# Thirty-six elementwise differences moved from VectorE to GpSimd in a fused MLP kernel

**Chip and metric.** One core of one Trainium2 chip. The metric is the device time of one execution in microseconds (us). All runs told here were in the fast state, save the single run of the last experiment, whose state is unknown; where a time is given, it is the median of a kernel's runs.

## The reference

Eight batches of 1024 rows go through two matrix products with a tanh GELU between them:

```python
# x: 8 x 1024 x 1024, w1: 1024 x 4096, w2: 4096 x 1024, all float32
h = x @ w1
h = 0.5 * h * (1 + np.tanh(np.sqrt(2 / np.pi) * (h + 0.044715 * h ** 3)))
return (h @ w2).astype(np.float32)
```

## The kernel before

The kernel works on blocks of 1024 rows (`sb` 0 to 7), in fp16, and computes both products by a Strassen-like scheme with seven products in place of eight. In a block, `matmul1` (m1) makes the GELU values `g` in four tiles, g11, g12, g21 and g22; the second matmul then needs sums and differences of these tiles, the first of which, g11 - g21, is made in m1, written over g21, two chunks (a "pair", `j`) at a time. A "later m1" is that of `sb` 2 to 7, in which two of the seven products are split once more ("inner").

Cut to what the change and the argument touch:

```python
def tt(out, in0, in1, op, pin=False):            # line 119 in every profile
    i = nc.vector.tensor_tensor(out=out, in0=in0, in1=in1, op=op)
    if pin:
        tc.keep_in_program_order(i)
...
        def add(out, in1, in0=None):             # in1 is a PSUM bank
            tt(out, out if in0 is None else in0, in1, ADD, True)
...
        def difference(j):
            if j >= 0:
                cs = slice(2 * j, 2 * j + 2)
                tt(g["21"][:, cs], g["11"][:, cs], g["21"][:, cs], SUB, True)
...
        def steady(j):
            ...   # pairs 0 to 3: GpSimd copies a mark from g11 ("pace"), then issues the loads of the next x
            if sb > 1 and j == 5:                # "early": a part of the second matmul, on GpSimd
                early[7] = gcp.tile([P, NI // 2, HT // 2], GT, name="gc")
                u, v = (inner_block(g["22"], b) for b in ("11", "21"))
                nc.gpsimd.tensor_tensor(out=early[7], in0=u, in1=v, op=SUB)
...
        for j in range(NI // 2):                 # 8 pairs
            ...   # products 1 and 2; gelu "21" of the pair before, on ScalarE
            for h in range(2):
                add(a[h], banks_b[h])
            difference(j - 1)
            ...   # products 5, 6, 3, 7, their adds and gelus
            steady(j)
        difference(NI // 2 - 1)
```

## Time and profile before

| | before |
|---|---|
| time, median of the three runs (range) | 1487.91 us (1487.71 to 1488.25) |
| TensorE (PE) busy | 1477.3 of 1486.0 us |
| VectorE (DVE) busy | 1149.5 us |
| GpSimd (POOL) busy | 231.8 us |
| one pair of a later m1, difference to difference | 11.73 us |
| VectorE busy in a later m1, from its first inner matmul to the second matmul (mean of six) | 61.7 of 86.9 us |

The line to read first is TensorE's: what is not 1477.3 us is mostly start-up.

How the rows read: a row in order of time has the start and the duration in us, engine, line, operation, output<-inputs, shapes, how many instructions are merged in it (x5), and in brackets the idle time of the engine in front of it and what ended that. A row of a list of waits has the total in us, how many times, and the longest. A row of the chain (the work that ended last, followed back) has only start, duration, engine, tile and line. L119 is the helper `tt`, so the tiles tell its rows apart; g is fp16 in SBUF, tmp fp32 in SBUF, ps a bank of PSUM.

### The profile page before, as it was taken

The page shows a single profiled execution, that of the slowest core. Times are in us where ns is not written, and L with a number is a line of the kernel's source. Part 1 is how long each engine was busy: PE and PEld are TensorE (multiplying, and loading weights), DVE is VectorE, ACT ScalarE, POOL GpSimd, SP SyncE. Part 2 cuts the span into 40 slices and gives each one's busy share as a digit, 9 for nine tenths or more (in the row PEclk, how much of TensorE's full clock was granted, in tenths as well). Part 3 has the DMA queues.
Part 4 walks back from the last instruction along what each step waited for, and adds up shares of the span by engine and source line. Part 5 has one row for each costly group of instructions (what it writes and reads, how often), then busy time and mean ns, then how long its engine had stood idle before and what let it go on. Part 6 is the DMA issues. An engine that isn't in the chain of part 4 may idle for free.

```text
span 1486.0 us, 26324 instructions
## 1 busy us (share of the span) xinstructions
PE 1477.3 (99%) x9879; PEld 964.2 (65%) x9879; DVE 1149.5 (77%) x1792; ACT 613.3 (41%) x1154; POOL 231.8 (16%) x311
## 2 busy tenths in 40 slices
PE   9999999999999999999999999999999999999998
PEld 5444444444455787558875588655886568855687
DVE  6657458767677898779987799877997779877887
ACT  5665026621166412663136621366214652056510
POOL 2542222222211012100022001210111101101011
PEclk9999999999999999999999999999999999999999
DMA  9999798987997999989999899998999989997886
GB/s 331 340 355 404 202 363 291 405 269 228 383 288 173 358 306 308 336 203 386 303 307 340 222 364 307 311 305 244 353 305 321 307 263 340 294 373 240 297 279 212
DMA packets 242719, 453.70 MB, mean 305 GB/s; under 512 B 80672, under 2 KB 85792, under 8 KB 241696
## 3 DMA queue, kind: packets, MB, share of 16 engines
q1 hardware_dynamic: 215680, 358.69, 71.6%
q0 software_dynamic: 26912, 93.34, 21.3%
q8 instruction: 77, 1.26, 0.3%
q14 instruction: 50, 0.41, 0.1%
HBM read 355.47 MB, written 111.15 MB: 314 GB/s over the span
## 4 chain that ended last, share of the span: by engine, by line
PE 97%; DVE 1%; DMA 1%; issue 0%; ACT 0%; DVEq 0%
PE ps L438 49%; PE ps L902 35%; PE ps L943 13%; PE ps L368 1%; DVE tmp L119 1%; DMA out_dram<-tmp 0%; PE ps L345 0%; DMA u<-in_x_dram 0%; DVE u L119 0%; ACT u L135 0%; ACT tmp L135 0%; PE ps L303 0%; DVE tmp L337 0%; DVE u L356 0%; DVEq L119 0%
## 5 line engine op out<-in xcount | busy, mean ns | idle before, releaser
L438 PE MATMUL ps<-u 128*128 128x512 f16 (+1 forms) x4104 | 746.7, 344 | 2.3 <-DVE tmp L119 2.3
L119 DVE TENSOR_TENSOR tmp<-tmp,ps 128x256 f32<-128x256 f32 (+1 forms) x930 | 450.7, 532 | 273.9 <-PE ps L438 169.4
L438 PEld LDWEIGHTS <-u 128*128 128x128 f16 x4104 | 401.1, 98 | 345.3 <-issue 11.0
L135 ACT COPY tmp<-ps 128x512 f32<-128x512 f32 x410 | 231.3, 581 | 302.1 <-PE ps L438 154.1
L451 ACT ACTIVATE g<-tmp 128x512 f16<-128x512 f32 x378 | 238.1, 633 | 165.2 <-DVE tmp L119 165.0
L902 PE MATMUL ps<-u,gc 128*128 128x256 f16 x2688 | 300.4, 273 | 0.0
L902 PEld LDWEIGHTS <-gc 128*128 128x128 f16 x2688 | 262.5, 98 | 31.2
L902 PE MATMUL ps<-u,g 128*128 128x256 f16 x2016 | 227.9, 273 | 0.0
L119 DVE TENSOR_TENSOR u<-u 128x2048 f16<-128x2048 f16 (+3 forms) x292 | 219.5, 790 | 9.2 <-DMA raw_d<-u 2.5
L135 ACT COPY u<-ps 128x512 f32<-128x512 f32 (+1 forms) x134 | 77.9, 587 | 348.9 <-PE ps L902 341.4
L902 PEld LDWEIGHTS <-g 128*128 128x128 f16 x2016 | 197.3, 98 | 24.1
L689 POOL DMA_DIRECT2D out_dram<-u x70 | 64.0, 989 | 710.5 <-issue 366.0
L119 DVE TENSOR_TENSOR u<-u,ps 128x512 f32<-128x512 f32 x216 | 147.7, 684 | 34.7 <-PE ps L902 28.5
L943 PE MATMUL ps<-u,g 128*128 128x512 f16 x768 | 166.4, 379 | 0.0
L943 PEld LDWEIGHTS <-g 128*128 128x128 f16 x768 | 75.1, 98 | 90.6
L119 DVE TENSOR_TENSOR g<-g,g 128x2048 f16<-128x2048 f16 (+1 forms) x136 | 130.3, 980 | 1.6 <-ACT g L451 1.6
L119 DVE TENSOR_TENSOR gc<-g,gc 128x2048 f16<-128x2048 f16 x84 | 102.4, 1219 | 0.6
L119 DVE TENSOR_TENSOR gc<-g 128x2048 f16<-128x2048 f16 x78 | 95.0, 1218 | 0.0
L451 ACT ACTIVATE g<-ps 128x512 f16<-128x512 f32 x134 | 79.9, 597 | 13.9 <-PE ps L438 6.9
L138 POOL CAST u<-gc 128x1024 f16<-128x1024 f32 x40 | 47.2, 1190 | 64.7 <-DMA gc<-in_w_dram 61.7
L415 POOL COPY pace<-g 128x2 f16<-128x2 f16 x24 | 4.4, 185 | 191.4 <-ACT g L451 191.4
L536 POOL TENSOR_TENSOR gc<-g 128x2048 f16<-128x2048 f16 x6 | 24.4, 4063 | 62.1 <-ACT g L451 62.1
(37 smaller groups left out, 257.3 us busy)
## 6 DMA issues: line engine op xcount, KB each, us to landing
u<-w_d SPq DMA_DIRECT2D x336, 256.0 KB, 6.5
u<-in_d SPq DMA_DIRECT2D x168, 512.0 KB, 7.1
u<-raw_d SPq DMA_DIRECT2D x252, 256.0 KB, 7.1
out_dram<-u POOLq DMA_DIRECT2D x70, 512.0 KB, 9.3
gc<-in_w_dram SPq DMA_DIRECT2D x48, 512.0 KB, 6.3
u<-in_d SPq DMA_DIRECT2D x96, 256.0 KB, 7.4
raw_d<-u SPq DMA_DIRECT2D x32, 512.0 KB, 8.9
u<-raw_d SPq DMA_DIRECT2D x32, 512.0 KB, 14.1
```

The costliest lines, as they stand in the source:

```text
L119: i = nc.vector.tensor_tensor(out=out, in0=in0, in1=in1, op=op)
L135: tc.keep_in_program_order(nc.scalar.copy(out=out, in_=in_))
L138: pool_last[0] = nc.gpsimd.tensor_copy(out=out, in_=in_)
L368: tc.keep_in_program_order(nc.tensor.matmul(bank[:, cols], lhsT=w[:, k, :], rhs=self.xs.blocks[f"{a}{r}"][:, k, cols], start=r == 1 and k ...
L415: mark = nc.gpsimd.tensor_copy(out=pace, in_=g_chunk[:, :2])
L438: tc.keep_in_program_order(nc.tensor.matmul(bank, lhsT=w, rhs=x, start=first and k == 0, stop=k == n - 1, skip_group_check=not first,))
L451: gelu_last[0] = nc.scalar.activation(out=g[b][:, c, :], in_=src, func=GELU)
L536: nc.gpsimd.tensor_tensor(out=early[7], in0=u, in1=v, op=SUB)
L689: return nc.gpsimd.dma_start(out=rows, in_=src, **kw)
L902: tc.keep_in_program_order(nc.tensor.matmul(bank[:, i * OH // 2:(i + 1) * OH // 2], lhsT=t[:, c, i * P:(i + 1) * P], rhs=self.y[j][:, c, : ...
L943: tc.keep_in_program_order(nc.tensor.matmul(pair(bank), lhsT=a[:, c, :], rhs=chunks(pieces[c // QC])[:, :, c % QC, :], start=(first and c ...
```

## The change

The intent: VectorE is the busiest engine behind TensorE, GpSimd is nearly idle in the later m1, so six of the eight differences of such an m1 go to GpSimd. The last two stay, since the second matmul starts right behind them.

```diff
         def difference(j):
             if j >= 0:
                 cs = slice(2 * j, 2 * j + 2)
-                tt(g["21"][:, cs], g["11"][:, cs], g["21"][:, cs], SUB, True)
+                if sb > 1 and j < NI // 2 - 2:
+                    tc.keep_in_program_order(nc.gpsimd.tensor_tensor(
+                        out=g["21"][:, cs], in0=g["11"][:, cs], in1=g["21"][:, cs], op=SUB,
+                    ))
+                else:
+                    tt(g["21"][:, cs], g["11"][:, cs], g["21"][:, cs], SUB, True)
```

## The prediction

> **What bounds the kernel now.** I read the page's first section first, then the chain that ended last, then the waits of TensorE alone, then the later first matmuls (m1) instruction by instruction. The first section and the list of TensorE's waits:
>
> ```profile
> PE 1477.3 (99%) x9879; PEld 964.2 (65%) x9879; DVE 1149.5 (77%) x1792; ACT 613.3 (41%) x1154; POOL 231.8 (16%) x311
> ```
> ```profile
> PE ps L438 <- DVE tmp L119: 2.3, 7, 0.6
> PE ps L303 <- DVE warm L1027: 1.2, 1, 1.2
> PE ps L345 <- DVE tmp L337: 0.7, 1, 0.7
> PE ps L368 <- ACT u L135: 0.6, 1, 0.6
> ```
>
> TensorE is taken for 1477.3 of 1486.0 us, and in the whole execution it waits for VectorE (DVE) 2.3 us in seven places; the other rows belong to the start-up. The chain says the same: 97% of it is PE, 1% is DVE. A busy TensorE need not be at its best rate, so I worked out a floor from two stretches of the chain that hold one width only:
>
> ```profile
> 208.71 96.69 PE ps L438 x448
> ...
> 856.80 85.63 PE ps L902 x784
> ```
>
> 448 matmuls of 512 columns in 96.69 us are 0.2158 us each; 784 of 256 columns in 85.63 us are 0.1092 us each. In the later m1 (sb 2 to 7) one pair of chunks is five plain products (2 chunks x 4 matmuls of 512 columns: 40 in all) and two inner ones (7 parts x 2 matmuls of 256 columns: 28 in all), which agrees with the 68 weight loads per pair that the timeline shows. At those rates a pair takes 40 x 0.2158 + 28 x 0.1092 = 11.69 us. The differences themselves give the period that is kept, since one comes per pair. On VectorE, in the m1 that runs from about 762 to 857 us:
>
> ```profile
> 801.06 2.40 DVE L119 TENSOR_TENSOR tmp<-tmp,ps 128x256 f32<-128x256 f32 x5 [0.95 <-PE ps L438]
> 803.38 0.68 DVE L119 TENSOR_TENSOR g<-g,g 128x1024 f16<-128x1024 f16 x1
> 804.69 0.42 DVE L119 TENSOR_TENSOR tmp<-tmp,ps 128x256 f32<-128x256 f32 x1 [0.63 <-ACT tmp L135]
> ...
> 812.79 2.40 DVE L119 TENSOR_TENSOR tmp<-tmp,ps 128x256 f32<-128x256 f32 x5 [0.95 <-PE ps L438]
> 815.11 0.68 DVE L119 TENSOR_TENSOR g<-g,g 128x1024 f16<-128x1024 f16 x1
> 816.42 0.42 DVE L119 TENSOR_TENSOR tmp<-tmp,ps 128x256 f32<-128x256 f32 x1 [0.63 <-ACT tmp L135]
> ```
>
> The period is 815.11 - 803.38 = 11.73 us, so 0.04 us of a pair is above the floor. Over 8 pairs x 6 such m1 that is about 2 us, all that any change to VectorE in this stage could win. The second thing in these rows matters more: behind each difference VectorE is idle for 0.63 us, waiting for a ScalarE copy. The add behind the difference does not start earlier if the difference is gone.
>
> **What the Trainium skill says.** The page "GPSIMD Engine Reference", section "3.1 Elementwise — side-by-side cycle accounting", gives 4497 ns on GpSimd against 2293 ns on VectorE for an add of 2048 fp32 elements. This trace has a GpSimd subtraction of that length in fp16 (line 536, the early part of the second matmul), and it takes 4063 ns, so a tenth less; VectorE takes 1219 ns for 2048 fp16 elements, so here the gap is more than three to one. The page "SBUF — State Buffer", section "Who interferes with whom", says that a VectorE instruction with two SBUF inputs contends with a GpSimd instruction that reads SBUF, whichever starts first blocking the other completely, while a VectorE instruction with at most one SBUF input does not contend (outside its two-port modes). The trace agrees with the harmless half:
>
> ```profile
> 810.02 4.06 POOL L536 TENSOR_TENSOR gc<-g 128x2048 f16<-128x2048 f16 x1 [3.29 <-ACT g L451]
> ```
>
> It lies from 810.02 to 814.08 us, across VectorE's adds at 811.42 and 812.79. These have one input in SBUF (tmp) and one in PSUM (ps), and they keep the 0.42 and 2.40 us of the pair before, quoted above. No VectorE instruction with two SBUF inputs falls into it, so nothing here shows the blocking half.
>
> **The change part by part.** Removed from VectorE: pairs 0 to 5 of each of six m1, 36 instructions at 0.684 us (that is what all of them take), 24.6 us. VectorE's sum goes from 1149.5 to about 1125, from 1792 to 1756 instructions. None of it is on the path, by the 0.63 us of idle time behind each.
>
> Added to GpSimd (POOL): 36 subtractions of 1024 elements. Half of line 536's 4063 ns is 2.03 us; with something fixed per instruction, my estimate is 2.1 us each, 75 us in all. POOL's sum goes to about 307 us, from 311 to 347 instructions, still only a fifth of the span.
>
> Moved in time: a difference on POOL need not stand behind VectorE's adds. Its input is the second gelu "21" of the pair before. For the difference at 803.38 that gelu is this one:
>
> ```profile
> 800.77 0.60 ACT L451 ACTIVATE g<-ps 128x512 f16<-128x512 f32 x1
> ...
> 805.32 0.18 POOL L415 COPY pace<-g 128x2 f16<-128x2 f16 x1 [10.32 <-ACT g L451]
> ```
>
> So POOL can begin at about 801.5 and end at about 803.6. Its next work, the mark that paces the loads of the next x, waits for a gelu "11" until 805.32 whatever comes before it; some 1.7 us remain. The loads start when they did. For pairs 3 to 5 POOL has only line 536 besides. That subtraction comes in program order with pair 5, behind the difference of pair 4, so it should begin near 827 instead of 810 us. Its result is used by the fifth step of the first product of the second matmul, 4 x 12.23 / 7 = 7.0 us after 856.8, so some 33 us after it would end (an estimate). The last POOL difference ends near 839 us, and the first VectorE readers of these blocks are the 128x2048 sums of g at about 871 us. Keeping the last two pairs on VectorE is what protects this: their differences stand at 850.31 and 858.28 us, right where the second matmul begins.
>
> The sum: 24.6 us less on an engine with idle time, 75 us more on an engine with more idle time, 0 on the path.
>
> **The rivals.** First, a real gain. VectorE is 71% busy in this stage (61.7 of 86.9 us in each), the second-busiest engine, so relief looks worthwhile. Against it: six of the seven TensorE waits for VectorE lie in pair 0 of an m1 (409.52, 589.78, 769.96, 949.88 us and so on), some 10 us before the first difference; the seventh is 0.16 us at 636.99 and its chain comes from a ScalarE copy with VectorE idle 0.91 us. Even with the whole 2 us, the time would be about 1486.
>
> Second, contention for the shared SBUF interface. If POOL's 2.1 us held up VectorE's adds each time, less the 0.63 us that are idle, 36 x 1.5 us would be up to 54 us, 1540 us. Against it speaks the one measured overlap above: the adds beside line 536 are not a nanosecond group longer. The adds have one SBUF input; the two-input instructions are the differences of pairs 6 and 7 and the four x sums in pair 0, all away from POOL's new work.
>
> Third, a new wait in POOL's queue. If a difference started later than I think, the mark and x loads behind it would slip, then the transposes, which share the SP queue with the weight loads. A slip of 2 us is covered by weights fetched up to three pairs of 11.73 us ahead. TensorE would feel it only if the slip added up, and it has no way to, since each difference is 2.1 us in a period of 11.73. I give this 1 to 3 us at worst.
>
> **Range and chances.** The three runs before span 0.54 us. I take 1487.8 us, no change. The low end, 1486.2, is most of the 2 us above the floor; the high end, 1489.4, allows some shift of DMA order and one new small wait per m1. Leaving within 2% means 30 us, which only full contention could bring: 2% for slower, 0.5% for faster (the floor forbids it).
>
> **What would show it.** Right: VectorE near 1125 us, POOL near 307; the 128x1024 group of g on VectorE 28 instead of 64; a POOL group of 36 at 2.0 to 2.2 us; the pace marks and x loads at the same places in their pairs; TensorE's waits for VectorE still near 2.3 us, m1's period still 11.73 us; the adds beside the POOL differences still 0.42 and 0.68 us, and the idle time behind the removed difference grown from 0.63 to about 1.3 us. Wrong: adds beside a POOL difference that take 1 to 2 us longer or start late, a period over 11.8 us, new rows in TensorE's waits, or the second matmul's first sums waiting for POOL.

## The result

The changed kernel took 1487.73 us (1487.65 to 1488.04, six runs), the kernel before 1488.15 us (1487.71 to 1488.64, six runs by then). The ratio is 0.9997, with a 95% interval of 0.9984 to 1.001: no difference. A ratio here is the mean time of one kernel's runs over that of the other's of the same rounds, so it is not quite the ratio of the medians quoted.

The first section of the changed kernel's page and its list of TensorE's waits:

```profile
PE 1477.2 (99%) x9879; PEld 964.3 (65%) x9879; DVE 1128.3 (76%) x1756; ACT 613.3 (41%) x1154; POOL 303.1 (20%) x347
```
```profile
PE ps L438 <- DVE tmp L119: 1.9, 7, 0.3
```

VectorE lost 21.2 us and GpSimd gained 71.3 us, and TensorE's row and its waits stayed where they were. The chain shows it in this block's m1, from its first inner matmul on, before and then after:

```profile
769.96 86.83 PE ps L438 x502
```
```profile
769.59 86.84 PE ps L438 x502
```

In time order on VectorE, the same place of the same block as in the prediction:

```profile
800.69 2.40 DVE L119 TENSOR_TENSOR tmp<-tmp,ps 128x256 f32<-128x256 f32 x5 [0.95 <-PE ps L438]
804.32 0.42 DVE L119 TENSOR_TENSOR tmp<-tmp,ps 128x256 f32<-128x256 f32 x1 [1.23 <-ACT tmp L135]
...
812.42 2.40 DVE L119 TENSOR_TENSOR tmp<-tmp,ps 128x256 f32<-128x256 f32 x5 [0.95 <-PE ps L438]
816.05 0.42 DVE L119 TENSOR_TENSOR tmp<-tmp,ps 128x256 f32<-128x256 f32 x1 [1.23 <-ACT tmp L135]
```

The row of the difference is gone, and the idle time in front of the next add has grown from 0.63 to 1.23 us, still ended by the same ScalarE copy. (All times in this block are 0.37 us earlier than before; that shift was there at its first pair, before any difference.) And GpSimd:

```profile
801.08 2.13 POOL L501 TENSOR_TENSOR g<-g,g 128x1024 f16<-128x1024 f16 x1 [6.41 <-ACT g L451]
804.94 0.18 POOL L415 COPY pace<-g 128x2 f16<-128x2 f16 x1 [1.74 <-ACT g L451]
805.39 1.01 POOL L410 DMA_DIRECT2D xb<-in_x_dram  x2 [0.26 <-issue]
809.65 4.06 POOL L541 TENSOR_TENSOR gc<-g 128x2048 f16<-128x2048 f16 x1 [3.25 <-ACT g L451]
813.67 2.12 POOL L501 TENSOR_TENSOR g<-g,g 128x1024 f16<-128x1024 f16 x1
824.54 2.13 POOL L501 TENSOR_TENSOR g<-g,g 128x1024 f16<-128x1024 f16 x1 [8.74 <-ACT g L451]
```

The difference at 801.08 lies across VectorE's five adds at 800.69, which keep their 2.40 us. The pace mark has 1.74 us of idle time in front of it, so the loads of x start at the same place in their pair. One thing is not as predicted: the early part (line 541 here, 536 before) still runs at 810 us, ahead of the difference of pair 3.

### The profile page after: what moved, and what is told of

Same layout as the page of the kernel before. It is cut to its first block, busy times and chain, and to the rows that moved or that the text cites. A ratio compares the mean times of both kernels' runs of the same rounds, so it can differ in the third digit from the quotient of the medians.

```text
span 1486.0 us, 26334 instructions
## 1 busy us (share of the span) xinstructions
PE 1477.2 (99%) x9879; PEld 964.3 (65%) x9879; DVE 1128.3 (76%) x1756; ACT 613.3 (41%) x1154; POOL 303.1 (20%) x347
## 4 chain that ended last, share of the span: by engine, by line
PE 98%; DVE 1%; issue 0%; DMA 0%; ACT 0%; DVEq 0%
PE ps L438 49%; PE ps L907 35%; PE ps L948 13%; PE ps L368 1%; DVE tmp L119 1%; PE ps L345 0%; DMA u<-in_x_dram 0%; ACT u L135 0%; PE ps L303 0%; DVE tmp L337 0%; DVE u L119 0%; ACT tmp L135 0%; DVE u L356 0%; DVEq L119 0%
## 5 line engine op out<-in xcount | busy, mean ns | idle before, releaser
L119 DVE TENSOR_TENSOR u<-u 128x2048 f16<-128x2048 f16 (+3 forms) x292 | 219.4, 790 | 21.2 <-DMA raw_d<-u 10.3
L501 POOL TENSOR_TENSOR g<-g,g 128x1024 f16<-128x1024 f16 x36 | 76.5, 2125 | 230.0 <-ACT g L451 220.4
L119 DVE TENSOR_TENSOR g<-g,g 128x2048 f16<-128x2048 f16 (+1 forms) x100 | 106.4, 1094 | 1.6 <-ACT g L451 1.6
L119 DVE TENSOR_TENSOR gc<-g,gc 128x2048 f16<-128x2048 f16 x84 | 102.4, 1219 | 0.6
L682 POOL DMA_DIRECT2D out_dram<-tmp x32 | 17.4, 544 | 92.2 <-DVE tmp L119 80.7
```

The source lines that it names most:

```text
L501: tc.keep_in_program_order(nc.gpsimd.tensor_tensor(out=g["21"][:, cs], in0=g["11"][:, cs], in1=g["21"][:, cs], op=SUB,))
L682: return nc.gpsimd.dma_start(out=out2[r0:r0 + P, o0:o0 + OH], in_=src, **kw)
```

## The experiments

The theory: the differences stood in a hole of VectorE's order (idle time that ends only when something else, here a ScalarE copy, is done) and not on the path, and on GpSimd they do no harm because the VectorE instructions beside them have one input in SBUF and one in PSUM. The rivals: a gain and an equal loss that cancel; or a GpSimd instruction that never disturbs VectorE, so that the exception for the last two pairs would be needless. "Spare" below is a VectorE subtraction g11 - g11 of 1024 fp16 elements into a tile that nobody reads.

### No difference at all (wrong result on purpose)

The edit as it looks against the changed kernel:

```diff
-                if sb > 1 and j < NI // 2 - 2:
-                    tc.keep_in_program_order(nc.gpsimd.tensor_tensor(...))
-                else:
+                if not (sb > 1 and j < NI // 2 - 2):
                     tt(g["21"][:, cs], g["11"][:, cs], g["21"][:, cs], SUB, True)
```

> Wrong result on purpose: the differences of pairs 0 to 5 of the later m1 are left out on every engine. Main theory (none of this work is on the path): 1487.7 us, within 0.1% of the changed kernel, m1's period still 11.73 us. Rival (the changed kernel gained by VectorE's relief and lost as much by GpSimd's new load): several us less, 1484 to 1486 us.

1487.81 us (1487.55 to 1488.71), ratio 0.9998 (0.9985 to 1.001). With the 36 differences on no engine the time is the same within that interval (some 2 us either way), and the stretch shown above takes 86.84 us here too: the work was worth nothing where it stood, and no pair of cancelling effects is seen. The GpSimd load costs nothing either, since the changed kernel is no slower than this one.

### One and three spare subtractions behind each difference on VectorE

In the kernel before:

```diff
                 tt(g["21"][:, cs], g["11"][:, cs], g["21"][:, cs], SUB, True)
+                for _ in range(1 if sb > 1 and j < NI // 2 - 2 else 0):      # 3 in the second kernel
+                    tt(spare, g["11"][:, cs], g["11"][:, cs], SUB, True)
```

> The kernel before (all differences on VectorE), with one spare VectorE subtraction of 0.68 us behind each of the 36 differences of pairs 0 to 5 of the later m1. Theory (the difference stands in a hole of about 1.23 us that ends with a ScalarE copy): the spare one fills what is left, 0.63 us, and the time stays within 0.1%, 1487 to 1489 us. Rival (VectorE work at this place is on the path in part, as the spare subtraction ahead of the adds was, which cost 12 us in 36 places): 1495 to 1500 us.

1487.82 us (1487.36 to 1488.39), ratio 0.9998 (0.9986 to 1.0011). VectorE's busy time went up to 1169.4 us and the time did not move. In its trace the hole is just filled; the last add has no idle time in front of it:

```profile
802.93 0.68 DVE L119 TENSOR_TENSOR g<-g,g 128x1024 f16<-128x1024 f16 x1
803.53 0.68 DVE L119 TENSOR_TENSOR spare<-g 128x1024 f16<-128x1024 f16 x1
804.24 0.42 DVE L119 TENSOR_TENSOR tmp<-tmp,ps 128x256 f32<-128x256 f32 x1
```

> The same with three spare subtractions behind each difference. Theory: 0.6 us are free, the other 1.2 us of each pair put off the add that TensorE's next inner part waits for; with some slack left there, 0.8 to 1.2 us per pair, 29 to 43 us in all, 1517 to 1531 us, with TensorE's waits for VectorE's tmp grown by as much. Rival (only VectorE's sum counts: 3.4 us idle per pair, 1.8 us added): 1488 us.

1536.54 us (1536.34 to 1536.97), ratio 1.0326: 48.6 us over the kernel before in those rounds (1487.99), 1.35 us for each of the 36 places, a little above the 0.8 to 1.2 expected. The rival by sums falls: VectorE was still only 79% busy. TensorE's list of waits shows who waits:

```profile
PE ps L438 <- DVE tmp L119: 45.0, 40, 1.6
```
```profile
811.62 0.41 DVE L119 TENSOR_TENSOR tmp<-tmp,ps 128x256 f32<-128x256 f32 x1
...
812.08 6.12 PE L438 MATMUL ps<-u 128*128 128x256 f16 x35 [1.22 <-DVE tmp L119]
```

The add behind the hole reads an inner product's bank that TensorE goes on accumulating into; TensorE starts 0.05 us after the add ends. The add starts 2.66 us after its difference (808.96 to 811.62), in place of the 1.31 us of the kernel before and of the one with one spare: 1.35 us late, just what each place costs. So the place has 0.6 us to spare, and beyond that VectorE's time is passed on to TensorE in full.

### A spare subtraction in the middle of GpSimd's difference, and its control

```diff
+            if sb > 1 and 0 < j < NI // 2 - 1:
+                tt(spare, g["11"][:, 0:2], g["11"][:, 0:2], SUB, True)
             for h in range(2):
                 add(a[h], banks_b[h])
             difference(j - 1)
```

The control has the same lines in the kernel without the differences of pairs 0 to 5.

> The control of the run before, wrong result on purpose: the same spare VectorE subtraction at the same place, and no difference of pairs 0 to 5 on any engine. Both theories: the spare subtraction takes 0.68 us, the time is 1487.7 us.

> The changed kernel with one spare VectorE subtraction of 1024 elements with two SBUF inputs (g11 minus g11 into a tile nobody reads), placed in front of the two last adds so that it falls into the middle of the GpSimd difference. Exclusion theory: the spare subtraction or the GpSimd one takes up to 1.5 us longer than alone (0.68 and 2.12 us), or shows idle time in front of it. Rival (no exclusion): 0.68 and 2.12 us as before. The time by both: 1487.7 to 1490 us, since VectorE has about 3.9 us of idle time in a pair; if the held-up adds reach TensorE, more.

The control took 1500.59 us (1499.97 to 1501.43), ratio 1.0082, 12 us more, which I had not expected: ahead of the adds even 0.6 us of VectorE time is partly on the path (TensorE waits 9.6 us for tmp, in place of 2.3), while behind them (the kernel with one spare) it is free. With the GpSimd difference beside it the kernel took 1542.35 us (1541.97 to 1542.78), ratio 1.0363. So the meeting itself costs 41.8 us, 1.2 us for each of 36 places on average. My upper end of 1490 us was far too low: I had counted VectorE's idle time over the pair instead of at this place. GpSimd and VectorE in that kernel, pairs 2 and 3 of a block:

```profile
822.63 2.12 POOL L501 TENSOR_TENSOR g<-g,g 128x1024 f16<-128x1024 f16 x1 [6.41 <-ACT g L451]
...
832.88 4.06 POOL L541 TENSOR_TENSOR gc<-g 128x2048 f16<-128x2048 f16 x1 [3.25 <-ACT g L451]
836.91 2.57 POOL L501 TENSOR_TENSOR g<-g,g 128x1024 f16<-128x1024 f16 x1
```
```profile
823.24 2.06 DVE L119 TENSOR_TENSOR spare<-g 128x1024 f16<-128x1024 f16 x1
825.22 1.27 DVE L119 TENSOR_TENSOR tmp<-tmp,ps 128x512 f32<-128x512 f32 x2
...
836.65 0.84 DVE L119 TENSOR_TENSOR spare<-g 128x1024 f16<-128x1024 f16 x1
```

In the first meeting GpSimd is ahead: the spare subtraction begins at 823.24, GpSimd ends at 824.75, and the spare one ends only at 825.30, so it takes 2.06 us in place of 0.68. In the second it is the other way: VectorE's waits for the early part to end at 836.94, and then GpSimd's difference, begun at 836.91, takes 2.57 in place of 2.12 us. Only the first kind costs time. Between spare subtractions that VectorE has to wait in lie 13.42 us (809.82 to 823.24), 1.37 more than in the control (12.05); from pair 3's to the next there are 12.20 us, as in the control. Five such places in each of six m1, 30 x 1.37, give 41.1 of the 41.8 us (an estimate from one block's spacing).

A held-up instruction shows as a longer one, not as idle time in front of it. The Trainium skill, page "SBUF — State Buffer", section "Who interferes with whom", says that a VectorE instruction with two SBUF inputs contends with a GpSimd one that reads SBUF; these runs agree, in both orders. The adds, with one SBUF input, are untouched in every kernel here (683 and 417 ns on average, within 2 ns). No run separates the number of SBUF inputs from the element type: each instruction held on VectorE is fp16 with both inputs in SBUF, each untouched one fp32 with one in PSUM. That the inputs decide is the page's statement.

### The spare subtraction behind the adds, in the hole

```diff
                 if sb > 1 and j < NI // 2 - 2:
                     tc.keep_in_program_order(nc.gpsimd.tensor_tensor(...))
+                    tt(spare, g["11"][:, cs], g["11"][:, cs], SUB, True)
```

> The changed kernel with the same spare two-SBUF subtraction on VectorE, but behind the two last adds, in the hole that the removed difference left. Main theory (place decides: the hole is 1.23 us and the GpSimd difference ends 0.2 us after the hole begins): the spare one starts near 803.0 us of its block, is held up by 0.1 to 0.6 us, ends before the ScalarE copy that ends the hole, and the time stays at 1487.7 us, where the same instruction 1.2 us earlier cost 54 us. Rival (any two-SBUF instruction in the pair costs): 1495 us or more.

1489.05 us (1489.02 to 1490.04), ratio 1.0009 (0.9995 to 1.0023), so by its interval not told apart from no change. The spare subtraction took 0.75 us at most places and 1.61 us at pair 3, where GpSimd's difference comes late behind the early part:

```profile
815.20 1.61 DVE L119 TENSOR_TENSOR spare<-g 128x1024 f16<-128x1024 f16 x1
816.74 0.41 DVE L119 TENSOR_TENSOR tmp<-tmp,ps 128x256 f32<-128x256 f32 x1
```

There it leaves the hole by about 0.2 us: at the other pairs that add starts 1.31 us after the spare subtraction, here 1.54. The chain runs through it, in this m1 and in three others:

```profile
770.05 42.74 PE ps L438 x248
...
815.29 0.80 DVE spare L119
...
817.20 39.90 PE ps L438 x230
857.10 85.63 PE ps L908 x784
```

From the first inner matmul of this m1 to the second matmul it has 87.05 us (770.05 to 857.10), in place of 86.84 in the changed kernel. Five of the six m1 are longer by 0.19 to 0.21 us in this way, 1.0 us in all, and the sixth (`sb` 3) is the same in both kernels, 87.11 us. That is most of the 1.2 us by which the medians differ, a difference that the times alone do not tell from noise. The same instruction 1.2 us earlier in the order cost 54 us: place decides.

### All eight pairs, and seven pairs, on GpSimd

```diff
-                if sb > 1 and j < NI // 2 - 2:
+                if sb > 1:                          # second kernel: sb > 1 and j < NI // 2 - 1
```

> GpSimd makes the differences of all eight pairs of the later m1, the last two as well. Main theory (a two-input GpSimd subtraction and a VectorE instruction with two SBUF inputs exclude each other): the last difference starts on GpSimd at about 857.1 us of the block that ends near 857, lasts 2.1 us, and the first sum into gc, which has two SBUF inputs and would like to start at 858.0, can finish only about 1.2 us after 859.2, at 860.4 instead of 859.7; TensorE's first matmuls from gc start about 0.7 us late in each of six blocks, so some 4 us more, about 1492 us, with new waits of TensorE for VectorE's gc. Rival (no exclusion, only the sums count): the gc sum keeps 1.22 us, ends earlier than before (859.2), and the time stays at 1487.7.

> GpSimd makes seven pairs, VectorE only the last. Theory (the 3.3 us of the all-pairs kernel come from the last difference alone, which holds up the first sum into gc): 1487.7 us, no waits of TensorE for gc. Rival (half of it comes from pair 6): about 1489.5 us.

All eight: 1491.68 us (1491.33 to 1491.94), ratio 1.0022 (1.001 to 1.0035). Seven: 1487.83 us (1487.52 to 1488.06), ratio 0.9998 (0.9985 to 1.001). The last difference alone costs the 3.3 us. In the all-pairs kernel, on GpSimd, VectorE and TensorE:

```profile
858.45 2.12 POOL L501 TENSOR_TENSOR g<-g,g 128x1024 f16<-128x1024 f16 x1 [7.00 <-ACT g L451]
...
859.22 2.44 DVE L119 TENSOR_TENSOR gc<-g,gc 128x2048 f16<-128x2048 f16 x1
...
861.72 6.50 PE L907 MATMUL ps<-u,gc 128*128 128x256 f16 x58 [0.48 <-DVE gc L119]
```

The first sum into gc has two SBUF inputs. It takes 2.44 in place of 1.22 us, ends 1.1 us after GpSimd, and TensorE waits 0.48 us for it in each of six blocks (2.9 us in its list of waits, where the changed kernel has no such row). That is the second rival of the prediction, made real. It is also why the exception in the change is needed, though for the last pair only.

### Every m1

```diff
-                if sb > 1 and j < NI // 2 - 2:
+                if j < NI // 2 - 2:
```

> The changed kernel without the condition on the later m1: GpSimd makes the differences of pairs 0 to 5 in sb 0 and 1 too, 12 more. There VectorE makes sums with two SBUF inputs in every pair. Exclusion theory: of 12 differences most meet such sums, these take up to 2 us longer where they start behind the GpSimd one, and GpSimd's casts of w1 in sb 0 and stores of sums in sb 1 are put off by 2 us each; VectorE has some 3 us idle in a pair of sb 1, so 0 to 20 us, 1488 to 1508 us. Rival (the exclusion does not matter there): 1487.7 us and unchanged durations.

1489.35 us (1488.69 to 1489.79), ratio 1.0008 (0.9994 to 1.0022). In `sb` 0 and 1 VectorE makes sums of 2048 elements in the pairs; the mean of that group, 1229 ns in the changed kernel, rose to 1358 ns over 88 instructions (11.4 us), so the exclusion is there, and nearly all of it falls into VectorE's idle time. The inner matmuls of `sb` 2 start at 410.63 us in its trace, and at 409.50 in the changed kernel's.

### The early part held in program order

```diff
-                nc.gpsimd.tensor_tensor(out=early[7], in0=u, in1=v, op=SUB)
+                tc.keep_in_program_order(nc.gpsimd.tensor_tensor(out=early[7], in0=u, in1=v, op=SUB))
```

> The changed kernel with the early part of the second matmul (GpSimd, 4.06 us) held in program order. Theory (it ran at 810 us, ahead of the difference of pair 3, because it is not held in order): now it starts behind the difference of pair 4, near 827 us; the time stays at 1487.7 us. Rival (its place comes from something else): it stays at 810 us.

One look, of a single run whose state is unknown: 1488.32 us. The early part now starts at 827.24 us, behind the difference of pair 4, as the prediction had placed it in the changed kernel, and the time is within what single runs of the others show. So it had run early because nothing held it.

## Why the prediction was right

**The bound and the floor.** Right. Nothing that took work off VectorE in the later m1 shortened the time, not even leaving the work out; in the chain, the stretch of a later m1 from its first inner matmul on took 86.83 or 86.84 us in five of the six m1, before and after, and 87.11 us in that of `sb` 3 both times.

**The 0.63 us of idle time behind each difference.** This was the step that carried the forecast, and it held: the hole grew to 1.23 us, one more subtraction in it was free, three were not.

**The costs.** GpSimd took 2125 ns for one difference, as estimated (2.1 us). VectorE's sum fell by 21.2, not by 24.6 us. The term that was mis-sized is the 0.684 us per instruction: neighbouring VectorE rows overlap (801.06 + 2.40 is 803.46, the difference starts at 803.38), and the busy time counts an overlap once, so one removed row takes away some 0.6 us. GpSimd's sum rose by 71.3 in place of 75 us: the differences brought 76.5, and one cast in `sb` 0 read 0.75 us in place of 5.5 (VectorE was busy without a break beside it in the kernel before, and in the changed kernel it met one sum; that this is the same hold is not shown).

**GpSimd's order.** The step "that subtraction comes in program order with pair 5" was wrong: the instruction was not held in order and stayed at 810 us, so that the difference of pair 3 started right behind it, at 813.67. It cost nothing, because nothing waits for that difference until the second matmul.

**The rivals.** The gain was none. The contention was right in kind and rightly ruled out by counting SBUF inputs: it appears as soon as a VectorE instruction with two SBUF inputs lies beside the GpSimd one, and two runs show that it reaches TensorE then. One reading was too narrow. "Nothing here shows the blocking half" holds for the later m1 that the prediction looked at, but the same trace of the kernel before has that half in `sb` 0, where GpSimd's casts of w1 meet VectorE's sums:

```profile
56.33 1.41 POOL L138 CAST u<-gc 128x1024 f16<-128x1024 f32 x1 [1.09 <-DVE tmp L119]
```
```profile
56.15 0.68 DVE L119 TENSOR_TENSOR g<-g,g 128x1024 f16<-128x1024 f16 x1
56.75 2.06 DVE L119 TENSOR_TENSOR u<-u 128x2048 f16<-128x2048 f16 x1
```

The cast begins while a VectorE difference runs and takes 1.41 in place of the 1.04 us of most casts; the VectorE sum begun at 56.75 takes 2.06 in place of 1.22 us and ends 1.07 us after the cast (57.74). So both orders could have been read before any run, and the cast and the difference share no tile. The 54 us that the prediction gave to full contention are near the 54 us of the kernel with the spare subtraction, but by chance: some 12 of those are the spare subtraction itself. The third rival, a slip of the pace marks, did not come: they kept 1.7 us.

## What to carry to other kernels

Before moving work off a busy engine, look at what ends the idle time behind each instance of it: if the next instruction waits for something else anyway, the move is worth nothing, however large the sum. Before giving elementwise work to GpSimd, count the SBUF inputs of the VectorE instructions that will run beside it: in these runs those with one input in PSUM kept their time, and those with two in SBUF were held until the GpSimd instruction ended, or held it when they came first. How much a place in an engine's order can bear is measured by putting spare work there, since the idle share of the whole stage does not tell it.

## What the Trainium skill lacked or had wrong

- "GPSIMD Engine Reference", sections 3.1 and 4.1: the only duration of a two-input elementwise instruction is for fp32 (4497 ns for 2048 elements), and GpSimd is called about twice as slow as VectorE for two inputs. In fp16 the runs show 2125 ns for 1024 elements and 4064 ns for 2048, against 684 and 1219 ns on VectorE: more than three times.
- "SBUF — State Buffer", section "Who interferes with whom": it agrees in kind, in both orders (0.68 to 2.06 us on VectorE, 2.12 to 2.57 us on GpSimd). It does not say how a profile shows the hold: as a longer instruction of the held engine and as no wait, so that a list of that engine's waits misses it.
- "Perfetto Trace Analysis", section "GPSIMD Engine Instruction", calls a GpSimd instruction's span in a profile unreliable and advises the spacing of starts. Here both agree: two neighbours start 4.02 us apart (809.65 and 813.67), and the first one's duration is 4.06 us.
